# State-space input weights built in (group, channel) layout, rotation tables built by VectorE and ScalarE

## Chip, cores, metric

The kernel runs on one core of a Trainium2 chip. The metric is the device time of one execution in microseconds (us). A "piece" below is one weight tile of 128 x 1024 (or 128 x 512) floats, with the products made from it.

## What is computed

The reference is a two-layer trunk over 272 rows (16 meta tokens, 256 tokens) of 2048 features. Layer 0 mixes with a gated linear recurrence and differential attention, layer 1 with an S5 state-space layer and RWKV-7; a SwiGLU feed-forward network (hidden 5632) follows each. The change touches only constants of the S5 layer, which depend on parameters and not on the rows:

```python
dt = exp(log_dt)[:, None]                       # (64 groups, 1)
mag = exp(lr * dt)                              # (64 groups, 64 states)
ar, ai = mag * cos(li * dt), mag * sin(li * dt)
den = lr * lr + li * li
cr = ((ar - 1) * lr + ai * li) / den
ci = (ai * lr - (ar - 1) * li) / den
bbr = cr[..., None] * br - ci[..., None] * bi   # (64, 64, 16 channels): input weights
bbi = cr[..., None] * bi + ci[..., None] * br
bu_r, bu_i = einsum('btgc,gpc->btgp', ug, bbr), ... bbi
h = scan(a = ar + i ai, bu);  y = Re(c h)       # 272 rows
```

The kernel turns the complex scan into two real ones by rotating with cos(n th), sin(n th) for n = 0..271, th = li * dt. These are the rotation tables: for each of 32 blocks of 128 states a 128 x 2 x 272 tile. Tables, input weights and output weights go to one DRAM tensor, `s5p`, from which layer 1 loads one 448 KB tile per block (`stab`).

## The kernel before

Nearly all work is a stream of dense products that `run_dense` writes out in one order: layer 0's mixing, its feed-forward network (FFN0), layer 1's mixing, its feed-forward network (FFN1). For each piece, `load_piece_` has SyncE's queue (SP) load the weights (`st`), ScalarE (ACT) round them to `hi` (line 161) and VectorE (DVE) form the rest `lo` (line 162). TensorE (PE) then makes three matmuls for each of 8 (or 4) blocks: hi with xhi, hi with xlo, lo with xhi (lines 195 to 197). `st`, `hi` and `lo` have three buffers each, so `hi` of a piece can only be written once PE is through with the piece three before.

In the feed-forward network a gate product is evacuated by DVE (`ga`, line 299), passed through Silu on ACT (300) and multiplied on GpSimd (POOL, 301); the up product is multiplied with it on DVE (`gu`, 310) and split by ACT and DVE (`ah`, `al`, 214 and 215). A down product is added to `h` on DVE (210). Products have two PSUM banks: the product after next waits for the evacuation. FFN0 starts with the norm's row factors: sums of squares on PE (256), `rs` on DVE (264), the power on POOL (`rr`, 266), a broadcast copy on DVE (`re`, 268), PE (`b`, 271) and a copy on ACT (`rb`, 273).

`s5_setup` gives steps that `build` hangs on items of FFN0: `f0[2 + 6 * i]["post"] = fn`. In order: `scalars` (small DVE operations 128 x 32, lines 610 to 657), `weights_b` (POOL, 666 to 675), `weights_c` twice (POOL, 685 and 686), `weights_t` eight times and `table` eight times. `weights_t` (701 to 705) masks on POOL (`snat`), transposes on PE into PSUM bank `c` (702; 64 transposes in all), copies on ACT (`sev`) and stores. `table` (716 to 739) doubles the cos/sin table on POOL, six operations a level (`stm`, `stb`), and stores it.

Each engine runs its instructions in a fixed order, which a scheduler of the framework sets when the kernel is built from the program order, priorities and the buffers. Products' loads and evacuations have a raised priority, the tables a lowered one, so that they fill the places between.

Of the kernel before, what the change touches and what calls it, by code (L numbers as in the profile page):

```python
# [9 lines left out]
F32 = mybir.dt.float32  # L10
# [7 lines left out]
T = 272  # L18
# [15 lines left out]
for _n, _w in [  # L34
    ("g_mix0", 16), ("g_ffn0", 16), ("g_mix1", 16), ("g_ffn1", 16), ("g_fin", 16),
    ("conv_w", 32), ("conv_b", 8), ("lru_ba", 8), ("lru_bx", 8), ("lru_lam", 8), ("subln", 1),
    ("s5_d", 8), ("glu_b", 8), ("mu", 28), ("w0", 8), ("a0", 8), ("kk", 8), ("ka", 8), ("rk", 8),
    ("ln_w", 8), ("ln_b", 8), ("s5_lr", 32), ("s5_li", 32), ("s5_dt", 32),
]:
    VEC[_n] = (NV, _w)  # L40
    NV += _w


def _constants():
# [33 lines left out]
    sm = np.zeros((128, 4, 8), np.float32)  # L78
    for sc in range(4):
        for g in range(2):  # L80
            sm[64 * g:64 * g + 64, sc, 2 * sc + g] = 1
    s5 = {"sm": sm.reshape(128, 32)}
# [14 lines left out]
class Net:  # L97
# [14 lines left out]
    # ---------------------------------------------------------------- set up  # L112
# [31 lines left out]
    # ------------------------------------------------------- dense machinery  # L144
# [20 lines left out]
    def run_dense(self, items, first=(), lead=0, ahead=2):  # L165
        """The products of the items in turn; those of the first `lead` items go piece by piece through all of them."""
# [55 lines left out]
    # ------------------------------------------------------------- rms norms  # L222
# [3 lines left out]
    def norm_chunk(self, k, gname, c0):  # L226
        """h chunk k is final: scaled split of it and its part of the sum of squares."""
# [48 lines left out]
    # ------------------------------------------------------------------- FFN  # L276
# [65 lines left out]
    # --------------------------------------------------------------- layer 0  # L342
# [93 lines left out]
    def attention(self, hd, q, k, v, yb):  # L436
# [21 lines left out]
        for j, (q0, n) in enumerate(QT):  # L458
# [37 lines left out]
            # mean of squares of the normalised row, its inverse root, and the factor of the row  # L496
# [12 lines left out]
    def lru_setup(self):  # L509
# [14 lines left out]
        # softplus(-lam), twice  # L524
# [52 lines left out]
    def gelu2(self, dst, x, pl, n):  # L577
        """dst = 2 gelu(x), in the form with tanh"""
# [8 lines left out]
    # --------------------------------------------------- layer 1, state space  # L587
    def s5_setup(self):
        """Steps that make the rotations, the input and the output weights, kept in DRAM."""
# [12 lines left out]
        def scalars():  # L602
            pl = st["pl"] = self.pool("s5s", 1, es)
            st["pl2"] = self.pool("s5s2", 2, es)
            self.s5c = self.load_const("s5", pl)
            st["b"] = self.t(pl, [128, 2, 32, 16], "sb")
            st["c"] = self.t(pl, [128, 2, 32, 16], "scc")
            nc.sync.dma_start(st["b"], self.I["s5_b"])
            nc.sync.dma_start(st["c"], self.I["s5_c"])
            x = {n: self.t(pl, [128, 32], "s_" + n) for n in  # L610
                 ("dt", "th", "n", "s", "sh", "c", "ar", "ai", "den", "cr", "ci", "t")}
            self.s5_rho = self.t(self.cp, [128, 32], "s_rho")
            lr, li = self.v("s5_lr"), self.v("s5_li")
            M, A, S = ALU.mult, ALU.add, ALU.subtract
            nc.scalar.activation(x["dt"], self.v("s5_dt"), AF.Exp)
            tt(x["t"], lr, x["dt"], M)
            nc.scalar.activation(self.s5_rho, x["t"], AF.Exp)
            tt(x["th"], li, x["dt"], M)
            # the angle within one turn
            V.tensor_scalar(x["n"], x["th"], 1.0 / (2 * math.pi), 12582912.0, op0=M, op1=A)  # L620
# [4 lines left out]
            for c in (c1, c2, c3):  # L625
                V.scalar_tensor_tensor(x["th"], x["n"], -c, x["th"], op0=M, op1=A)
            pi = 3.1415925
            V.tensor_scalar(x["th"], x["th"], pi, -pi, op0=ALU.min, op1=ALU.max)
            nc.scalar.activation(x["s"], x["th"], AF.Sin)
            nc.scalar.activation(x["sh"], x["th"], AF.Sin, scale=0.5)  # L630
            tt(x["c"], x["sh"], x["sh"], M)
            V.tensor_scalar(x["c"], x["c"], -2.0, 1.0, op0=M, op1=A)
            tt(x["ar"], self.s5_rho, x["c"], M)
            tt(x["ai"], self.s5_rho, x["s"], M)
            tt(x["den"], lr, lr, M)
            tt(x["t"], li, li, M)
            tt(x["den"], x["den"], x["t"], A)
            V.reciprocal(x["den"], x["den"])
            V.tensor_scalar(x["ar"], x["ar"], 1.0, None, op0=S)
            tt(x["cr"], x["ar"], lr, M)  # L640
            tt(x["t"], x["ai"], li, M)
            tt(x["cr"], x["cr"], x["t"], A)
            tt(x["cr"], x["cr"], x["den"], M)
            tt(x["ci"], x["ai"], lr, M)
            tt(x["t"], x["ar"], li, M)
            tt(x["ci"], x["ci"], x["t"], S)
            tt(x["ci"], x["ci"], x["den"], M)
            st["x"] = x
# [668 lines left out]
```

## Time and profile before

| | us |
|---|---|
| median of 3 runs | 2692.41 |
| runs | 2690.05 to 2692.90 |
| span of the profiled execution (the only time that its page gives) | 2690.4 |
| busy in the span: PE / DVE / ACT / POOL | 2582.8 / 1663.2 / 1161.8 / 878.0 |

The page gives the busy time of each engine, the span in 40 slices with the TensorE clock granted in each, the chain that ended last, and groups of instructions by line. A matmul of 272 columns reads as some 0.29 us although the next one starts 0.125 us later, since they are pipelined; so the pace of PE is read from starts and from counts in a stretch, and its busy time only tells when it did nothing.

### The profile page before, as it was taken

The page shows a single profiled execution, that of the slowest core. Times are in us where ns is not written, and L with a number is a line of the kernel's source. Part 1 is how long each engine was busy: PE and PEld are TensorE (multiplying, and loading weights), DVE is VectorE, ACT ScalarE, POOL GpSimd, SP SyncE. Part 2 cuts the span into 40 slices and gives each one's busy share as a digit, 9 for nine tenths or more (in the row PEclk, how much of TensorE's full clock was granted, in tenths as well). Part 3 has the DMA queues.
Part 4 walks back from the last instruction along what each step waited for, and adds up shares of the span by engine and source line. Part 5 has one row for each costly group of instructions (what it writes and reads, how often), then busy time and mean ns, then how long its engine had stood idle before and what let it go on. Part 6 is the DMA issues. An engine that isn't in the chain of part 4 may idle for free. (4 is left out here: it accounts for less than half of the span.)

```text
span 2690.4 us, 50770 instructions
## 1 busy us (share of the span) xinstructions
PE 2582.8 (96%) x20136; PEld 2490.8 (93%) x20136; DVE 1663.2 (62%) x2515; ACT 1161.8 (43%) x1852; POOL 878.0 (33%) x1417
## 2 busy tenths in 40 slices
PE   8999998888899999999999989999999999999998
PEld 7999998888899999999978778799999999999997
DVE  7666767445454555556678888755755555555555
ACT  5555544333334333334444434454544434343444
POOL 3110316999831010001166776740210101010103
PEclk9999999899899999999999999999999999999999
DMA  5444455546556555555554434333555655555554
GB/s 190 141 143 142 154 177 176 172 155 215 174 183 197 177 173 175 178 173 173 186 173 150 143 121 134 98 102 117 172 188 173 190 187 185 185 188 184 185 187 143
DMA packets 160189, 447.86 MB, mean 166 GB/s; under 512 B 34960, under 2 KB 51024, under 8 KB 159824
## 3 DMA queue, kind: packets, MB, share of 16 engines
q1 hardware_dynamic: 143376, 442.32, 51.6%
q10 hardware_dynamic: 16576, 2.30, 0.5%
q8 instruction: 159, 2.61, 0.4%
q14 instruction: 78, 0.64, 0.1%
HBM read 421.69 MB, written 22.87 MB: 165 GB/s over the span
## 5 line engine op out<-in xcount | busy, mean ns | idle before, releaser
L161 ACT CAST hi<-st 128x1024 fp32r<-128x1024 f32 (+1 forms) x776 | 793.1, 1023 | 1152.1 <-PE p L196 822.1
L162 DVE TENSOR_TENSOR lo<-st,hi 128x1024 fp32r<-128x1024 f32 (+1 forms) x776 | 955.9, 1232 | 518.0 <-ACT hi L161 514.2
L195 PE MATMUL p<-xhi,hi 128*128 128x272 f32 (+1 forms) x4256 | 1238.8, 291 | 26.0 <-ACT hi L161 15.7
L197 PE MATMUL p<-xhi,lo 128*128 128x272 f32 (+1 forms) x4256 | 1239.2, 291 | 7.8 <-DVE lo L162 7.8
L196 PE MATMUL p<-xlo,hi 128*128 128x272 f32 (+1 forms) x4256 | 1235.5, 290 | 0.0
L195 PEld LDWEIGHTS p<-xhi,hi 128*128 128x128 f32 x4256 | 812.2, 191 | 39.7 <-issue 21.3
L197 PEld LDWEIGHTS p<-xhi,lo 128*128 128x128 f32 x4256 | 815.1, 192 | 21.9 <-issue 10.8
L196 PEld LDWEIGHTS p<-xlo,hi 128*128 128x128 f32 x4256 | 813.4, 191 | 11.1 <-issue 10.4
L301 POOL TENSOR_TENSOR ga<-ga,rb 128x272 f32<-128x272 f32 (+1 forms) x88 | 116.3, 1321 | 949.6 <-ACT ga L300 949.6
L195 PE MATMUL p<-ah,hi 128*128 128x272 f32 (+1 forms) x1408 | 403.3, 286 | 1.9 <-DVE gu L310 1.9
L197 PE MATMUL p<-ah,lo 128*128 128x272 f32 (+1 forms) x1408 | 403.2, 286 | 0.0
L196 PE MATMUL p<-al,hi 128*128 128x272 f32 (+1 forms) x1408 | 402.7, 286 | 0.0
L195 PEld LDWEIGHTS p<-ah,hi 128*128 128x128 f32 x1408 | 266.8, 189 | 2.1 <-issue 2.1
L197 PEld LDWEIGHTS p<-ah,lo 128*128 128x128 f32 x1408 | 266.9, 190 | 0.0
L196 PEld LDWEIGHTS p<-al,hi 128*128 128x128 f32 x1408 | 266.1, 189 | 0.0
L210 DVE TENSOR_TENSOR h<-p,h 128x256 f32<-128x256 f32 (+1 forms) x272 | 116.9, 430 | 155.6 <-PE p L197 154.6
L247 POOL TENSOR_TENSOR acc<-acc,sq 128x272 f32<-128x272 f32 (+1 forms) x56 | 60.7, 1084 | 261.8 <-ACT sq L242 261.3
L310 DVE TENSOR_TENSOR gu<-p,ga 128x272 f32<-128x272 f32 (+1 forms) x88 | 38.1, 433 | 120.2 <-PE p L197 73.9
L299 DVE TENSOR_TENSOR ga<-p,rb 128x272 f32<-128x272 f32 (+1 forms) x88 | 38.0, 432 | 54.7 <-PE p L197 54.7
L788 POOL TENSOR_TENSOR sx<-stab,sz 128x256 f32<-128x256 f32 x64 | 59.5, 932 | 26.6 <-DVE sz L785 11.0
L1078 POOL TENSOR_TENSOR xt<-ls,xs 40x15 f32<-40x15 f32 (+7 forms) x120 | 47.5, 396 | 49.5 <-DMA ls<-ld 43.1
L501 POOL TENSOR_TENSOR fs<-ss,mhalf 96x1 f32<-96x1 f32 (+1 forms) x24 | 13.3, 555 | 116.0 <-DVE ss L500 115.9
(378 smaller groups left out, 2835.6 us busy)
## 6 DMA issues: line engine op xcount, KB each, us to landing
st<-in_w_gate SPq DMA_DIRECT2D x176, 512.0 KB
st<-in_w_up SPq DMA_DIRECT2D x176, 512.0 KB
st<-in_w_down SPq DMA_DIRECT2D x160, 512.0 KB
st<-in_w_ev_in SPq DMA_DIRECT2D x80, 512.0 KB
st<-in_w_od_in SPq DMA_DIRECT2D x72, 512.0 KB
st<-in_w_ev_out SPq DMA_DIRECT2D x32, 512.0 KB
stab<-s5p SPq DMA_DIRECT2D x32, 448.0 KB
s5p<-stb SPq DMA_DIRECT2D x8, 1088.0 KB
```

The costliest lines, as they stand in the source:

```text
L161: nc.scalar.copy(hi[:, :kc], st[:, :kc])
L162: nc.vector.tensor_tensor(lo[:, :kc], st[:, :kc], hi[:, :kc].bitcast(F32), op=ALU.subtract)
L195: nc.tensor.matmul(p[:, :n], hi[:, o + k], xa, start=kk == 0, stop=False)
L196: nc.tensor.matmul(p[:, :n], hi[:, o + k], xb, start=False, stop=False)
L197: nc.tensor.matmul(p[:, :n], lo[:, o + k], xa, start=False, stop=kk == tot - 1)
L210: self.nc.vector.tensor_tensor(self.h[:, m, c0:], p, self.h[:, m, c0:], op=ALU.add)
L247: nc.gpsimd.tensor_tensor(self.acc[:, c0:], self.acc[:, c0:], sq[:, c0:], op=ALU.add)
L299: nc.vector.tensor_tensor(a[:, :n], p, self.rb[:, :n], op=ALU.mult)
L301: nc.gpsimd.tensor_tensor(a[:, :n], a[:, :n], self.rb[:, :n], op=ALU.mult)
L310: nc.vector.tensor_tensor(u[:, :n], p, a[:, :n], op=ALU.mult)
L788: (V if i == 3 else G).tensor_tensor(pr[i], a[:, NM:], b[:, NM:], op=M)
L1078: G.tensor_tensor(o, ls[:, s + 1:, s].unsqueeze(1).to_broadcast([40, j, n]), xs[:, :j, s:s + 1].to_broadcast([40, j, n]), op=M)
```

## The change

- The input weights are made in a layout of (group, channel) on the partitions and states along the row. The host lays out `lr`, `li` (repeated over the 16 channels), `br`, `bi` that way (`s5_q`, 1 MB in place of 0.5 MB), so the factors cr, ci are computed on 128 x 512 instead of 128 x 32 (`factors`), and no transpose is needed. `weights_t` is gone: its 64 transposes, 128 POOL operations, 16 ACT copies and 8 stores.
- `weights_b` masks the two groups on ACT (`seh`) and DVE (`sel`) and stores in 16 DMAs, each from 32 partitions.
- `weights_c` runs on ACT (12 activations) instead of POOL.
- The first 32 columns of all tables are made at once on DVE (`small`); each of 8 `table` steps copies them and makes the last four levels with, for each of 4 blocks, two ACT activations (`str`) and one DVE operation (`stb`).
- Steps stand 10 items apart instead of 6. Comments are removed (with that, and the new code, line numbers shift).

```diff
+        def factors():
+            x = {n: self.t(pl, [128, 512], "q_" + n) for n in ("th", "n", "s", "c", "t")}
...
+            tt(e(x["th"]), e(li), dt, M)
+            factor(x, x["th"])
+            nc.scalar.activation(x["s"], x["th"], AF.Sin)
+            nc.scalar.activation(x["th"], x["th"], AF.Sin, scale=0.5)
+            cos_of(x["c"], x["th"])
+            tt(e(x["t"]), e(lr), dt, M)
+            nc.scalar.activation(x["t"], x["t"], AF.Exp)
...
+            V.reciprocal(den, den)
...
+            nc.scalar.copy(inv, den)
...
         def weights_b():
+            for g in range(2):
+                m = hm[:, g:g + 1]
+                nc.scalar.activation(eh[:, :, :, g], bb, AF.Copy, scale=m)
+                V.scalar_tensor_tensor(el[:, :, :, g], bb, m, eh[:, :, :, g].bitcast(F32), op0=M, op1=S)
+            par = self.s5_par.rearrange("(c s) p w -> s p c w", s=4)
+            for i, x in enumerate((eh, eh, el, el)):
+                for sc in range(4):
+                    nc.sync.dma_start(par[sc, 32 * i:32 * i + 32, :, 2 * T:2 * T + 256],
+                                      x[32 * sc:32 * sc + 32].rearrange("p c m g s -> p c (m g s)").bitcast(F32))
+            st["es2"].close()
+            st["pl2"] = self.pool("s5s2", 2, es)
...
-        def weights_t(c):
-                    for sc in range(4):
...
-                            nc.gpsimd.tensor_tensor(n[:, 2 * i:2 * i + 2], src, hm, op=ALU.mult)
-                        nc.tensor.transpose(p[:, 128 * sc:128 * sc + 128], n.rearrange("p s a b -> p (s a b)"),
-                                            self.base["ident"])
-                    nc.scalar.copy(ev[:, :, m], p.rearrange("p (a b) -> p a b", a=4))
...
+        def small():
+            for lv in range(5):
+                n = 1 << lv
...
+                tt(a, co, C, M)
+                tt(b, si, Sn, M)
+                tt(tb[:, :, 0, n:2 * n], a, b, S)
+                tt(a, si, C, M)
+                tt(b, co, Sn, M)
+                tt(tb[:, :, 1, n:2 * n], a, b, A)
...
         def table(g):
-                        G.tensor_tensor(a, co, C, op=ALU.mult)
-                        G.tensor_tensor(b, si, Sn, op=ALU.mult)
...
+                tb = self.t(st["pl2"], [128, 4, 2, T], "stb")
+                V.tensor_copy(tb[:, :, :, :32], st["small"][:, 4 * g:4 * g + 4])
+                for lv, n in ((5, 32), (6, 64), (7, 128), (8, 256)):
                     w = min(n, T - n)
+                    for i in range(4):
+                        j = 4 * g + i
+                        t = self.t(st["pl2"], [128, 2, 128], "str")
+                        nc.scalar.activation(t[:, 0, :w], tb[:, i, 1, :w], AF.Copy, scale=st["nsin"][:, lv, j:j + 1])
+                        nc.scalar.activation(t[:, 1, :w], tb[:, i, 0, :w], AF.Copy, scale=st["pw"][:, lv, 1, j:j + 1])
+                        V.scalar_tensor_tensor(tb[:, i, :, n:n + w], tb[:, i, :, :w], st["pw"][:, lv, 0, j:j + 1],
+                                               t[:, :, :w], op0=M, op1=A)
...
-        steps += [weights_t(c) for c in range(8)] + [low(table(g)) for g in range(8)]
+        steps = [scalars, factors, weights_b, weights_c(0), weights_c(1), small]
+        steps += [low(table(g)) for g in range(8)]
...
-                f0[2 + 6 * i]["post"] = fn
+                f0[2 + 10 * i]["post"] = fn
```

How the order of instructions moves, at three places. The first is DVE's queue in FFN0 from the norm's broadcast copy `re` on (`lo` belongs to the weight pieces; `s_`, `spw` are 128 x 32 values of `scalars`). Before:

```order
L268 COPY re<-rr 68x512
L600 TENSOR_TENSOR s_t<-s_ai,vec 128x32
L600 TENSOR_TENSOR s_ci<-s_ai,vec 128x32
L632 TENSOR_SCALAR s_c<-s_c 128x32
L600 TENSOR_TENSOR s_ar<-s_rho,s_c 128x32
L651 COPY spw<-s_c 128x32
```

Now (`q_` are the 128 x 512 values of `factors`, `stq` and `stm` belong to `small`), and, some 60 instructions later, the reciprocal:

```order
L266 COPY re<-rr 68x512
L598 TENSOR_TENSOR q_th<-sq_5266,q_dt 128x512
L598 TENSOR_TENSOR q_t<-sq_5266,q_dt 128x512
L598 TENSOR_TENSOR s_t<-spw 128x32
...
L160 TENSOR_TENSOR lo<-st,hi 128x1024
L598 TENSOR_TENSOR stq<-stm_7944,stm_7945 128x32x4
L670 TENSOR_SCALAR q_c<-q_c 128x512
L669 RECIPROCAL q_n<-q_n 128x512
L598 TENSOR_TENSOR q_th<-q_s,sq_5266 128x512
L160 TENSOR_TENSOR lo<-st,hi 128x1024
```

Operations sixteen times as wide, and the steps of `small`, now stand between the `lo` of consecutive pieces; it goes on so for 22 pieces.

The second place is SP's queue, where the input weights are stored. Before, one of the eight stores among the weight loads:

```order
L158 DMA st<-in_w_down 128x512 x9
L705 DMA s5p<-sev 128x4x256
L158 DMA st<-in_w_down 128x512 x6
L739 DMA s5p<-stb 128x4x544
```

Now, all sixteen, in FFN0's second slice:

```order
L708 DMA s5p<-seh 32x8x256 x2
L156 DMA st<-in_w_up 128x1024
L708 DMA s5p<-seh 32x8x256 x6
L708 DMA s5p<-sel 32x8x256 x2
L156 DMA st<-in_w_up 128x1024
L708 DMA s5p<-sel 32x8x256
L156 DMA st<-in_w_gate 128x1024
L708 DMA s5p<-sel 32x8x256 x2
L156 DMA st<-in_w_gate 128x1024
L708 DMA s5p<-sel 32x8x256 x3
L156 DMA st<-in_w_up 128x1024 x2
```

The stores that were spread over FFN0 now stand together, with four weight loads among them.

The third place is DVE's queue in FFN0's first down product, whose pieces are 128 x 512 (`h` is the evacuation of a product). Before:

```order
L162 TENSOR_TENSOR lo<-st,hi 128x512
L210 TENSOR_TENSOR h<-p,h 128x272
L162 TENSOR_TENSOR lo<-st,hi 128x512
L210 TENSOR_TENSOR h<-p,h 128x272
```

Now, at its eleventh to thirteenth evacuation:

```order
L160 TENSOR_TENSOR lo<-st,hi 128x512
L755 SCALAR_TENSOR_TENSOR stb<-stb,spw,str 128x2x64
L208 TENSOR_TENSOR h<-p,h 128x272
L755 SCALAR_TENSOR_TENSOR stb<-stb,spw,str 128x2x64
L747 COPY stb<-stq 128x8x32
L755 SCALAR_TENSOR_TENSOR stb<-stb,spw,str 128x2x64
L208 TENSOR_TENSOR h<-p,h 128x272
L755 SCALAR_TENSOR_TENSOR stb<-stb,spw,str 128x2x128 x2
L208 TENSOR_TENSOR h<-p,h 128x272
L160 TENSOR_TENSOR lo<-st,hi 128x512
```

Table operations, each waiting for ACT, now stand between `lo` and `h`, and once the evacuations of the 11th, 12th and 13th product stand ahead of the `lo` of the 14th.

## Rows read from the trace of the kernel before

**Rows 1.** Busy time by stretch: FFN0's first 2496 matmuls, its other 3840; FFN1's start.
```profile
core 0: us, PE busy (x) PEld busy (x) DVE busy (x) ACT busy (x) POOL busy (x), PEclk, DMA share, GB/s
412.86:803.80 390.94, 346.94 (x2584) 342.19 (x2583) 207.20 (x267) 137.55 (x177) 315.77 (x619) 0.93 0.56 180
803.80:1286.37 482.57, 482.57 (x3845) 482.57 (x3843) 266.07 (x311) 195.31 (x239) 49.95 (x41) 1.00 0.56 178
1919.95:2058.28 138.33, 138.33 (x1164) 138.33 (x1165) 73.58 (x88) 59.87 (x77) 18.49 (x15) 1.00 0.55 176
2082.58:2173.95 91.37, 91.37 (x768) 91.37 (x769) 49.41 (x56) 38.72 (x48) 11.72 (x8) 1.00 0.61 191
```
**Rows 2.** Waits 412.86:803.8 of PE, DVE, SP: total us, times, longest.
```profile
PE c L702 <- POOL snat L701: 18.1, 7, 6.1
PE p L195 <- ACT hi L161: 7.1, 2, 4.9
...
PE b L271 <- DVE re L268: 4.8, 1, 4.8
...
DVE gu L310 <- POOL ga L301: 45.0, 10, 8.3
...
SPq L739 <- POOL stb L735: 26.3, 4, 9.1
```
**Rows 3.** PE in order of time, after the norm: start, us, instruction.
```profile
421.97 0.28 PE L196 MATMUL p<-xlo,hi 128*128 128x272 f32 x1
427.03 1.95 PE L271 MATMUL b<-c_base,re 68*128 68x68 f32 x8 [4.78 <-DVE re L268]
428.73 0.57 PE L197 MATMUL p<-xhi,lo 128*128 128x272 f32 x1
...
431.15 0.43 PE L195 MATMUL p<-xhi,hi 128*128 128x272 f32 x1
431.57 0.29 PE L197 MATMUL p<-xhi,lo 128*128 128x272 f32 x1
```
**Rows 4.** The same stretch on DVE, POOL and ACT.
```profile
416.31 0.35 DVE L638 RECIPROCAL s_den<-s_den 128x32 f32<-128x32 f32 x1
419.77 7.12 DVE L268 COPY re<-rr 68x512 f32<-68x512 f32 x1 [0.29 <-POOL rr L266]
428.10 1.23 DVE L162 TENSOR_TENSOR lo<-st,hi 128x1024 fp32r<-128x1024 f32 x1
429.25 0.18 DVE L600 TENSOR_TENSOR s_cr<-s_cr,s_den 128x32 f32<-128x32 f32 x1
...
419.71 6.89 POOL L685 TENSOR_TENSOR scw<-scc,c_base 128x256 f32<-128x256 f32 x12
...
417.55 1.28 ACT L629 ACT_TABLE_LOAD   x1
418.84 0.23 ACT L629 ACTIVATE s_s<-s_th 128x32 f32<-128x32 f32 x1
```
**Rows 5.** Instructions of line 268: duration in ns, min/median/max.
```profile
L268 DVE COPY re<-rr x5: 293/424/7116, 36.8 to 2677.8; 68x512 f32<-68x512 f32 x3, 128x256 f32<-128x256 f32 x2
```
**Rows 6.** Groups by line over the span: count | busy us, mean ns.
```profile
L300 ACT ACTIVATE ga<-ga 128x272 f32<-128x272 f32 x44 | 18.8, 428 | 15.0 <-DVE ga L299 15.0
L162 DVE TENSOR_TENSOR lo<-st,hi 128x512 fp32r<-128x512 f32 x48 | 34.4, 716 | 10.8 <-ACT hi L161 9.1
L210 DVE TENSOR_TENSOR h<-p,h 128x272 f32<-128x272 f32 x128 | 56.2, 439 | 78.1 <-PE p L197 77.8
L702 PE MATMUL c<-c_base,snat 128*128 128x128 f32 x64 | 16.8, 296 | 18.3 <-POOL snat L701 18.1 <-POOL stb L717 0.2
```
**Rows 7.** Busy time in a stretch of 2 us, columns as in the first group.
```profile
724.00:726.00 2.00, 2.00 (x11) 2.00 (x10) 0.00 (x0) 0.59 (x1) 0.87 (x4) 0.50 1.02 311
```
**Rows 8.** ACT's casts in 412.86:803.8 by shape: count | busy us, mean ns.
```profile
L161 ACT CAST hi<-st 128x1024 fp32r<-128x1024 f32 x96 | 100.5, 1049 | 153.4 <-PE p L196 93.3 <-DMA st<-in_w_up 17.4 <-DMA st<-in_w_gate 17.1
L161 ACT CAST hi<-st 128x512 fp32r<-128x512 f32 x16 | 9.9, 621 | 20.6 <-PE p L196 12.6 <-DMA st<-in_w_down 5.5 <-DVE lo L162 0.9
```

More of the change, by code (lines that the diff above doesn't have):

```diff
@@ L597, in s5_setup, with factor @@
         V = nc.vector
+        M, A, S = ALU.mult, ALU.add, ALU.subtract
         def tt(o, a, b, op):
             V.tensor_tensor(o, a, b, op=op)
[L602 to L620, printed above, removed]
+        def factor(x, th):
+            V.tensor_scalar(x["n"], th, 1.0 / (2 * math.pi), 12582912.0, op0=M, op1=A)
             V.tensor_scalar(x["n"], x["n"], 12582912.0, None, op0=S)
@@ new lines, in scalars @@
+        def scalars():
+            pl = st["pl"] = self.pool("s5s", 1, es)
+            st["es2"] = ExitStack()
+            st["plq"] = self.pool("s5q", 1, st["es2"])
+            self.s5c = self.load_const("s5", pl)
+            st["c"] = self.t(pl, [128, 2, 32, 16], "scc")
+            nc.sync.dma_start(st["c"], self.I["s5_c"])
+            st["q"] = self.t(st["plq"], [128, 4, 512], "sq4")
+            nc.sync.dma_start(st["q"], self.I["s5_q"])
+            x = {n: self.t(pl, [128, 32], "s_" + n) for n in ("dt", "th", "n", "sh", "t")}
+            self.s5_rho = self.t(self.cp, [128, 32], "s_rho")
+            lr, li = self.v("s5_lr"), self.v("s5_li")
+            pw = st["pw"] = self.t(pl, [128, 9, 2, 32], "spw")
+            nc.scalar.activation(x["dt"], self.v("s5_dt"), AF.Exp)
+            tt(x["t"], lr, x["dt"], M)
+            nc.scalar.activation(self.s5_rho, x["t"], AF.Exp)
+            tt(x["th"], li, x["dt"], M)
+            factor(x, x["th"])
+            nc.scalar.activation(pw[:, 0, 1], x["th"], AF.Sin)
+            nc.scalar.activation(x["sh"], x["th"], AF.Sin, scale=0.5)
+            cos_of(pw[:, 0, 0], x["sh"])
@@ new lines, in weights_b @@
+        def weights_b():
+            pl = st["plq"]
+            bb = st["bb"]
+            hm = self.s5c["hq"]
+            eh = self.t(pl, [128, 8, 2, 2, 64], "seh", F32R)
+            el = self.t(pl, [128, 8, 2, 2, 64], "sel", F32R)
+            for g in range(2):
[9 more added lines that the diff above has]
+            st["pl2"] = self.pool("s5s2", 2, es)
@@ L686, in f @@
-                nc.gpsimd.tensor_scalar(cw[:, :, 2], cw[:, :, 2], -1.0, None, op0=ALU.mult)
+                        sg = self.base["hm"][:, g:g + 1] if i < 2 else self.s5c["hn"][:, g:g + 1]
+                        nc.scalar.activation(cw[:, :, i, g], st["c"][:, m, 16 * half:16 * half + 16], AF.Copy, scale=sg)
                 nc.sync.dma_start(self.s5_par[16 * half:16 * half + 16, :, 2 * T + 256:].rearrange("j p c -> p j c"),
@@ L740, in f @@
+                nc.sync.dma_start(self.s5_par[4 * g:4 * g + 4, :, :2 * T].rearrange("j p c -> p j c"),
                                   tb.rearrange("p j a t -> p j (a t)"))
             return f
-        steps = [scalars, weights_b, weights_c(0), weights_c(1)]
         def low(fn):
```

153 lines of the change are left out of this document (61 added, 92 removed).

## Prediction

> **What bounds the kernel now.** I read the table by stretch first [rows 1]. PE sets the end: in FFN0's later 3840 matmuls it is busy in all of 482.57 us, 0.1257 us a matmul, at a granted clock of 1.00, while DVE works 266 us and ACT 195 us of it. Nothing off PE counts there. The same network's first 2496 matmuls, the stretch in which the state-space constants are made, take 390.94 us. At 0.1257 they would take 313.7. So **77.3 us** are lost, and that is all the change can reach. In it POOL is busy 316 of 391 us, PE idles 390.94 - 346.94 = 44.0 us, and the clock is 0.93.
>
> Then the waits of that stretch [rows 2]. PE waits longest for `snat`, the masks that POOL makes for the transposes (18.1 us). The others look like DVE or ACT being late, but POOL is behind them: DVE stood 45.0 us before `gu`, for the Silu product that POOL had queued behind table operations, and SP stood 26.3 us before a table's store, with weight loads queued behind it.
>
> Third, one stall in order of time [rows 3, 4]. PE stops for 4.78 us at the norm's row factors until DVE's `re` is there. `re` took 7.12 us, from 419.77, while POOL ran twelve operations from 419.71 for 6.89 us; its median is 0.424 us [rows 5]. [...]
>
> **The change part by part.** *Removed:* transposes, masks and tables on POOL, thus every wait in [rows 2] that ends on POOL, the slow `re`, and SP's wait for POOL. I take all 77.3 us as gone and add back what takes its place. Five terms.
>
> 1. The norm at FFN0's start. FFN1 has the same norm with nothing beside it: its first 1152 matmuls take 138.33 us where 1152 x 91.37 / 768 = 137.1 are plain [rows 1]. So 1.3 us are the floor. ACT now loads function tables three times there instead of twice, and does the exponential of `q_t` ahead of `rb`. A load took 1.28 us, and the activation behind it started right at its end [rows 4]. I take 2 us; ends 1.3 and 5.
>    [...]
>
> 2. `factors` and `small` on DVE, over 22 pieces, 22 x 24 x 0.1257 = 66 us of PE. Old work there: `lo` 1.23 us a piece and, every four pieces, `ga`, `gu` and `al`, each about as long as the evacuation `h` of the same shape, 0.44; together 34 us. To that come some 40 small steps of `scalars` at 0.18, 7 us [rows 4, 6]. New: about 30 operations of 512 columns, between half of a 1024-column `lo` and the 128 x 512 one, 0.61 to 0.72 us, 20 us; two of 1024 columns, 2.5; 30 steps of `small` from 0.18 to 0.72, 11; and the reciprocal. A 128 x 32 reciprocal took 0.35 against 0.18 of a product, 0.17 more for 32 columns, so about 3.3 us at 512 [rows 4]. Sum 78 us by durations. But each instruction starts about 0.08 us before the one ahead ends (428.10 + 1.23 against 429.25 [rows 4]), and there are some 150: 66 us. DVE then just keeps PE's pace, with the reciprocal as its worst lump. DVE normally finishes a piece's `lo` 6.0 - 1.05 - 1.23, or 3.7 us, before PE needs it. So between 0 and (78 - 66) - 3.7 + 1.2 = 9.5 us; I take 3, since the overlap is plain in the rows.
>
> 3. The sixteen stores. The first waits for `seh`, which ACT writes in about 2.5 us behind the `hi` of FFN0's 24th piece, 1.05 us, once PE is through with the 21st. The load behind the last store is the 31st piece's. PE then has pieces 22 to 30, 9 x 3.02 = 27.1 us, less 3.6 and less `hi` and `lo` of the 31st, 2.3: 21.2 us. To move in it: 16 x 32 x 8 x 256 x 4 bytes = 4.19 MB and four loads of 0.52, 6.29 MB. With its DMA engines full the kernel moved 311 GB/s [rows 7], which gives 20.3 us. It just fits; I take 1 us. DVE's first table copy waits for these stores too, with the same piece's `lo` behind it: the same deadline. Ends 0 and, at half that rate for the stores, 14 (below). SP's sixteen issues stand only beside its own slack.
>
> 4. FFN0's first down product. The `lo` of its 14th product now stands behind the evacuation of the 13th, so PE must stop: 0.44 + 0.72 us [rows 6], less two matmuls that need only `hi`, plus 1.2 at half clock: 2 us.
>
> 5. The rest of the table steps, 54 pieces (38 long, 16 short: 138 us of PE). ACT: casts 38 x 1.05 + 16 x 0.62 = 50 us [rows 8], 19 Silu and `ah` at 0.43, 8 us; and 256 new activations of 16 to 128 columns. Nearest rows: 0.23 us at 32 columns [rows 4], 0.43 at 272 [rows 6]; by width (60 columns in the mean) 0.25, 65 us. Sum 123 of 138 us. At 0.43 it would be 168, 30 too many. DVE has 136 short operations there, about 30 us, beside some 70 of its own. What may cost is the chain DVE to ACT to DVE, each link behind a `hi` that waits for PE. I take 3 us; ends 0 and 30.
>
> Layer 1's tail is reordered a little by the scheduler with the same instructions: 0, ends -4 and +4. Free POOL time elsewhere is worth nothing. Sum of what comes back: 2 + 3 + 1 + 2 + 3 = 11. **Gain 77.3 - 11 = 66 us.** The span was 2690.4, inside the range of the runs and 2.0 under their median, so I subtract from the median: 2692.4 - 66 = **2626 us**.
>
> **Rivals.** *The stores are slow.* Their source is 32 partitions, not 128. If such a transfer moves at half of 311 GB/s, the stores take 27.0 us and the loads among them 6.8, 33.8 against 21.2: PE stands 12.6 us, and 1.2 more at half clock, 13 above the 1 counted: 2639. Against it: two or more of them are under way at once, from different partitions. [...] Chance 0.14.
>
> *ACT becomes the bound in the table steps*, by term 5 at up to 30 us, less the 3 counted: up to 2653, likelier half of it, 2640. For it: 256 activations and their waits. Against: 0.23 us is the nearest row. Chance 0.13.
>
> *Slower.* The same chain, if it decides: to lose the 77 us the 54 pieces would need 138 + 77 = 215 us of ACT, less 58 for the old work, so 0.61 us for each of the 256 activations, waits included; above that the kernel is slower than before. At 0.65 it is 2692 - 66 - 3 + (58 + 166 - 138) = 2709. Rows at 0.23 and 0.43 speak against it. Chance 0.03.
>
> *The change doesn't free PE*: the weight stream, and not POOL, makes the early waits (ACT's `hi` waited 34.5 us for loads [rows 8]), and only the `snat` waits (18.1 us) and the transposes, at most their 16.8 us [rows 6], go: 2692 - 35 = 2657. Against it: the DMA share is 0.56 in both stretches of FFN0 [rows 1], with no wait in the later. Chance 0.04; nothing gained at all, 0.01.
>
> **The numbers.** My forecast has 0.65. Its own range goes from the floor (only 1.3 us come back, layer 1 gains 4: 2692 - 76 - 4 = 2612) to terms 2 and 3 at their ends. The range 2612 to 2656 takes in both rivals that end faster and leaves out the slower one, half of the last and some of the tails. No change means within 0.2%, 5.4 us, which a measurement of this kernel can hardly tell apart. Faster 0.96, same 0.01, slower 0.03, from the cases above.
>
> **What would show it.** Right: FFN0's first 2496 matmuls in 320 to 330 us, clock above 0.97, POOL nearly idle, no wait before `gu` on POOL, `re` at 0.4 us, one short PE stop in the first down product. Term 2 wrong: PE waiting for `lo` some 12 pieces into FFN0, behind the reciprocal. Term 3 wrong: one long stop near the 31st piece, with ACT waiting for a load or DVE for a store. Term 5 wrong: many short stops with DVE waiting for `str`. The forecast as a whole is wrong if FFN0's later 3840 matmuls change, or if layer 1 shifts by more than 4 us.

## The result

The changed kernel takes **2627.89 us** (median of 4 runs, 2625.61 to 2631.55) beside 2691.23 us of the kernel before in the same comparison: ratio 0.9773, 95% interval 0.9758 to 0.9789. The forecast was 2626 us, in a range of 2612 to 2656. The profiled execution has a span of 2624.0 us, 66.4 under that of before.

The two traces laid side by side, by the starts of the dense matmuls:

| stretch | before, us | changed, us | difference |
|---|---|---|---|
| up to FFN0 | 412.9 | 413.4 | +0.5 |
| FFN0's first 2496 matmuls | 390.9 | 331.7 | **-59.2** |
| FFN0's other 3840 | 482.6 | 484.2 | +1.7 |
| layer 1's mixing | 633.6 | 627.2 | -6.4 |
| FFN1 to the end of the span | 770.4 | 767.5 | -2.9 |

The changed kernel's busy time by stretch, columns as in [rows 1]; the rows answer to its first, second, third and fourth, with layer 1's mixing between:

```profile
413.38:745.09 331.71, 323.99 (x2522) 321.33 (x2521) 240.79 (x452) 198.72 (x437) 29.72 (x23) 0.98 0.67 217
745.09:1229.32 484.23, 484.23 (x3843) 484.23 (x3842) 266.00 (x311) 194.71 (x238) 49.61 (x38) 1.00 0.53 174
1229.32:1856.49 627.17, 598.20 (x4322) 527.23 (x4321) 476.08 (x776) 286.23 (x576) 340.49 (x597) 0.98 0.45 139
1856.49:1994.15 137.66, 137.66 (x1164) 137.66 (x1165) 73.59 (x88) 59.86 (x77) 18.44 (x15) 1.00 0.54 177
2018.43:2109.36 90.93, 90.93 (x769) 90.93 (x769) 49.41 (x56) 38.45 (x48) 11.70 (x8) 1.00 0.59 192
```

In the first row POOL's 315.77 us are down to 29.72, PE idles 331.71 - 323.99 = 7.7 us instead of 44.0, and the clock is 0.98 instead of 0.93. DVE and ACT carry the work, and PE doesn't notice it, but for four places. The waits of PE and DVE in this stretch (total, times, longest; against [rows 2]):

```profile
PE p L195 <- DVE lo L160: 4.1, 4, 2.5
PE p L193 <- ACT hi L159: 3.4, 3, 2.6
...
DVE stb L747 <- DMA s5p<-stb: 2.7, 2, 1.9
DVE stb L755 <- ACT str L754: 2.2, 6, 0.5
...
DVE gu L308 <- POOL ga L299: 1.0, 2, 0.7
```

The 45.0 us before `gu` have become 1.0. The norm's copy is back at its usual length (against [rows 5]), and PE has no stop there:

```profile
L266 DVE COPY re<-rr x5: 294/423/424, 35.7 to 2612.0; 68x512 f32<-68x512 f32 x3, 128x256 f32<-128x256 f32 x2
```

**Where the rest lies.** The stretch still takes 331.7 - 313.7 = 18 us more than its matmuls. Cut at PE's stops:

```profile
413.38:449.50 36.12, 35.95 (x288) 35.14 (x287) 31.35 (x83) 24.79 (x41) 6.44 (x3) 1.00 0.73 233
449.50:460.00 10.50, 8.01 (x52) 7.79 (x51) 10.50 (x22) 3.48 (x5) 1.79 (x1) 0.84 0.41 122
...
500.00:513.00 13.00, 9.95 (x56) 9.41 (x55) 3.56 (x5) 3.99 (x5) 0.77 (x1) 0.74 1.01 331
...
591.00:594.00 3.00, 2.21 (x15) 1.77 (x15) 2.98 (x8) 2.80 (x8) 0.00 (x0) 1.00 0.34 131
594.00:610.00 16.00, 14.78 (x113) 14.12 (x112) 11.60 (x26) 12.40 (x36) 0.77 (x1) 1.00 0.89 301
```

A row counts the matmuls under way, two or three more than start in it. From the starts: the norm 36.12 - 261 x 0.1257 (its 24 small matmuls left out) = 3.3 us; the stop at 450, 10.5 - 49 x 0.1257 = 4.3; the one at 502, 13 - 54 x 0.1257 = 6.2; the first down product 1.4; behind it 2.0; the stretches left out and the last 135 us together 0.8. Two stops make more than half of it. In the row from 449.50 DVE is busy all the time; in that from 500.00 the DMA engines are (share 1.01).

The first, on DVE in order of time:

```profile
445.73 1.21 DVE L160 TENSOR_TENSOR lo<-st,hi 128x1024 fp32r<-128x1024 f32 x1
446.86 0.28 DVE L598 TENSOR_TENSOR stq<-stm,stm 128x128 f32<-128x128 f32 x1
447.07 0.41 DVE L670 TENSOR_SCALAR q_c<-q_c 128x512 f32<-128x512 f32 x1
447.40 3.34 DVE L669 RECIPROCAL q_n<-q_n 128x512 f32<-128x512 f32 x1
...
451.51 1.21 DVE L160 TENSOR_TENSOR lo<-st,hi 128x1024 fp32r<-128x1024 f32 x1
```

PE's matmul with that second `lo` starts at 452.77, 2.77 us behind the one ahead of it. The second stop, on SP's queue (an SP row's duration is the time that the queue spent on issuing):

```profile
487.97 0.82 SPq L708 DMA_DIRECT2D s5p<-seh  x2
488.89 0.55 SPq L156 DMA_DIRECT2D st<-in_w_up  x1
489.49 6.46 SPq L708 DMA_DIRECT2D s5p<-seh  x6
496.05 1.85 SPq L708 DMA_DIRECT2D s5p<-sel  x2
497.99 0.71 SPq L156 DMA_DIRECT2D st<-in_w_up  x1
498.75 1.11 SPq L708 DMA_DIRECT2D s5p<-sel  x1
499.96 0.42 SPq L156 DMA_DIRECT2D st<-in_w_gate  x1
500.43 1.40 SPq L708 DMA_DIRECT2D s5p<-sel  x2
501.93 0.61 SPq L156 DMA_DIRECT2D st<-in_w_gate  x1
502.58 2.63 SPq L708 DMA_DIRECT2D s5p<-sel  x3
```

The sixteen stores occupy SP for 0.82 + 6.46 + 1.85 + 1.11 + 1.40 + 2.63 = 14.3 us. The load issued at 497.99, behind ten of them, is that of FFN0's 28th piece; its `hi` on ACT:

```profile
504.24 1.04 ACT L159 CAST hi<-st 128x1024 fp32r<-128x1024 f32 x1 [3.54 <-DMA st<-in_w_up]
```

PE starts that piece at 505.33, 2.90 us after its last matmul of the 27th.

### The profile page after: what moved, and what is told of

Its sections match the earlier page's. It is cut to its first block, busy times and chain, and to the rows that moved or that the text cites. A ratio compares the mean times of both kernels' runs of the same rounds, so it can differ in the third digit from the quotient of the medians.

```text
span 2624.0 us, 50534 instructions
## 1 busy us (share of the span) xinstructions
PE 2558.7 (98%) x20072; PEld 2467.8 (94%) x20072; DVE 1698.1 (65%) x2700; ACT 1221.0 (47%) x2111; POOL 591.2 (23%) x820
## 5 line engine op out<-in xcount | busy, mean ns | idle before, releaser
L160 DVE TENSOR_TENSOR lo<-st,hi 128x1024 fp32r<-128x1024 f32 (+1 forms) x776 | 936.4, 1207 | 489.8 <-ACT hi L159 485.8
L299 POOL TENSOR_TENSOR ga<-ga,rb 128x272 f32<-128x272 f32 (+1 forms) x88 | 126.1, 1433 | 1231.5 <-ACT ga L298 1231.5
L806 POOL TENSOR_TENSOR sx<-stab,sz 128x256 f32<-128x256 f32 x64 | 63.5, 995 | 27.6 <-DVE sz L803 10.5
L218 DVE SCALAR_TENSOR_TENSOR xlo<-h,vec,xhi 128x272 fp32r<-128x272 f32 (+1 forms) x64 | 50.7, 800 | 0.6 <-ACT xhi L217 0.5
```

Source lines behind the costliest of these rows:

```text
L160: nc.vector.tensor_tensor(lo[:, :kc], st[:, :kc], hi[:, :kc].bitcast(F32), op=ALU.subtract)
L218: nc.vector.scalar_tensor_tensor(lo, src, g, hi.bitcast(F32), op0=ALU.mult, op1=ALU.subtract)
L299: nc.gpsimd.tensor_tensor(a[:, :n], a[:, :n], self.rb[:, :n], op=ALU.mult)
L806: (V if i == 3 else G).tensor_tensor(pr[i], a[:, NM:], b[:, NM:], op=M)
```

## The experiments

Stretches are those of the table above, each from one profile (two where there are two numbers); each ratio is to the kernel before in the same comparison.

| run | FFN0's first 2496 | layer 1's mixing | median, us | ratio, 95% interval |
|---|---|---|---|---|
| before; again (one run) | 390.9; 388.9 | 633.6; 632.5 | 2691.2; 2687.8 | 1 |
| tables only | 338.3 | 637.1 | 2642.9 | 0.9829 (0.9805 to 0.9852) |
| weights only | 375.3 | 635.4 | 2675.6 | 0.9953 (0.9936 to 0.9969) |
| weights_c only | 384.2 | 627.3 | 2681.5 | 0.9974 (0.9965 to 0.9984) |
| ga on VectorE | 399.0 | 634.6 | 2697.4 | 1.0027 (1.0009 to 1.0046) |
| changed; again | 331.7; 327.9 | 627.2; 631.1 | 2627.9; 2627.0 | 0.9773; 0.9774 (0.9753 to 0.9794) |
| no reciprocal | 328.6 | 637.0 | 2626.4 | 0.9764 (0.9748 to 0.9781) |
| reciprocal spread; again | 324.6; 325.7 | 638.7; 634.5 | 2629.9; 2630.3 | 0.9779; 0.9778 (0.9764 to 0.9794) |
| fewer stores | 323.3 | 641.6 | 2631.4 | 0.9785 (0.9772 to 0.9799) |
| spread and fewer stores | 323.9 | 639.5 | 2630.8 | 0.9783 (0.9769 to 0.9797) |
| activations twice | 330.2 | 629.2 | 2626.2 | 0.9765 (0.9750 to 0.9780) |

### One part of the change at a time

Tables only: `small` and `table` of the changed kernel in the kernel before (`weights_c`'s tile moves with them to the pool with one buffer).

```diff
-        steps = [scalars, weights_b, weights_c(0), weights_c(1)]
+        steps = [scalars, weights_b, weights_c(0), weights_c(1), small]
...
         steps += [weights_t(c) for c in range(8)] + [low(table(g)) for g in range(8)]
```

> Only the tables go to VectorE and ScalarE; masks, transposes and weights_c stay as before. Theory (GpSimd's one queue is the jam, and tables and masks share in it): the waits of gu and of SP's stores on GpSimd go, the 18.1 us at snat shrink to about half, the transposes and the slow re stay; FFN0's first 2496 matmuls take 349 to 369 us instead of 391, the kernel 22 to 42 us less than before. Rival 1 (masks and transposes make nearly all of the loss): at most 15 us less. Rival 2 (the tables make nearly all of it): 55 us less or more.

Measured: -52.6 us in the stretch (against the second profile of before -50.6), -46.6 in the median; between the theory's range and the second rival's. The tables made most of the loss. PE's waits there:

```profile
PE p L197 <- DVE lo L162: 6.2, 4, 4.7
PE p L195 <- DVE gu L310: 2.1, 1, 2.1
PE p L195 <- ACT hi L161: 1.0, 1, 1.0
PE c L705 <- POOL snat L704: 1.0, 2, 0.9
```

Masks and transposes are all still there, and the 18.1 us of [rows 2] at `snat` are 1.0. So the masks were late because of the table operations on POOL, in whose queue they stood. The expectation was wrong on `re`: it took 0.42 us here, with `weights_c` still on POOL (below).

Weights only: the changed kernel with `table` of the kernel before and without `small`.

```diff
-        steps = [scalars, factors, weights_b, weights_c(0), weights_c(1), small]
+        steps = [scalars, factors, weights_b, weights_c(0), weights_c(1)]
```

> Only the input and output weights are made the new way; the tables stay on GpSimd, 10 items apart. Theory: the snat waits (18.1 us), the transposes (about 10) and the slow re (6) go, the norm, the reciprocal and the stores cost some 9 of it again, and gu still waits for GpSimd: 20 to 40 us less than before, FFN0's first 2496 matmuls in 351 to 371 us. Rival 1 (masks and transposes make nearly all of the loss): 50 us less or more. Rival 2 (the tables do): at most 10 us less.

Measured: -15.7 us in the stretch, -13.9 in the median, under the theory's range and above the second rival's. The parts overlap little: 52.6 + 15.7 = 68 against the 57 to 63 of the whole; by the medians 46.6 + 13.9 = 60.5 against 62.5. This run also shows how POOL slows DVE. One `lo`, in order of time, and the busy time of its stretch:

```profile
522.21 13.61 DVE L160 TENSOR_TENSOR lo<-st,hi 128x1024 fp32r<-128x1024 f32 x1
```
```profile
522.19:535.75 13.56, 2.28 (x19) 2.06 (x17) 13.56 (x3) 2.41 (x3) 12.55 (x18) 0.66 0.00 0
```

The operation takes 1.21 to 1.23 us elsewhere. POOL ran eighteen table operations without a pause beside it, and PE stood for some 11.4 of the 13.6 us. The kernel before does the same. Its second profile has this, with `ga` on POOL in the middle of the train:

```profile
546.44 12.58 DVE L162 TENSOR_TENSOR lo<-st,hi 128x1024 fp32r<-128x1024 f32 x1 [1.61 <-ACT hi L161]
```

PE waited 7.4 us for it. In the profile shown ahead the longest `lo` of this stretch is 2.06 us: where such a hold falls changes from one execution to the next.

Weights_c only, in the kernel before:

```diff
-                        nc.gpsimd.tensor_tensor(cw[:, :, i, g], src[:, :, g], hm[:, :, g], op=ALU.mult)
-                nc.gpsimd.tensor_scalar(cw[:, :, 2], cw[:, :, 2], -1.0, None, op0=ALU.mult)
+                        sg = self.base["hm"][:, g:g + 1] if i < 2 else self.s5c["hn"][:, g:g + 1]
+                        nc.scalar.activation(cw[:, :, i, g], st["c"][:, m, 16 * half:16 * half + 16], AF.Copy, scale=sg)
```

> The kernel before, with weights_c alone on ScalarE, so that the twelve 128 x 256 operations no longer run on GpSimd beside re. Theory (re took 7.12 us because GpSimd's long operations ran back to back beside it): re takes under 1.5 us, the pause at the norm goes, 4 to 8 us less than before. Rival (whatever GpSimd runs next holds re as long): re stays above 3 us and the gain is 0 to 3 us.

Measured: -6.8 us in the stretch against the first profile of before and -4.7 against the second, -7.9 in the median; `re` is back at 0.42 us:

```profile
419.89 0.42 DVE L268 COPY re<-rr 68x512 f32<-68x512 f32 x1 [0.28 <-POOL rr L266]
```

POOL's next operations had 4 columns here. The theory's numbers are met, but this run can't credit them to `re`: the second profile of the kernel before, `weights_c` on POOL as ever, has `re` at 0.42 us too, with the stop at the norm gone:

```profile
418.94 0.42 DVE L268 COPY re<-rr 68x512 f32<-68x512 f32 x1 [0.29 <-POOL rr L266]
419.34 8.12 POOL L685 TENSOR_TENSOR scw<-scc,c_base 128x256 f32<-128x256 f32 x12 [0.44 <-DMA scc<-in_s_c]
```

There POOL waited 0.44 us for a load, so its twelve operations began 0.40 us behind `re`; they took 8.12 us instead of 6.89. Where they began 0.06 us ahead of it ([rows 4], and the run with `ga` on VectorE below), `re` took 7.12 and 7.19 us. So what held `re` was a train of long POOL operations that had begun before it, and that one stop comes and goes between executions; the whole stretch was only 2 us shorter without it. At 431.8 of this run PE waits 4.67 us for `ga`. The gain of 7.9 us in the median is clear of the noise (ten executions against fourteen); which of POOL's fewer operations brings it isn't shown.

### Is it POOL's queue, or POOL beside DVE?

```diff
-                nc.gpsimd.tensor_tensor(a[:, :n], a[:, :n], self.rb[:, :n], op=ALU.mult)
+                (nc.gpsimd if layer else nc.vector).tensor_tensor(a[:, :n], a[:, :n], self.rb[:, :n], op=ALU.mult)
```

> The kernel before, with the product behind FFN0's Silu (ga) on VectorE instead of GpSimd, and all constants still made on GpSimd. Theory (the loss is the wait in GpSimd's queue: 45 us of VectorE before gu): these waits go, PE's stops at hi, gu, ga and lo shrink, 15 to 30 us less than before. Rival (the loss is GpSimd's operations holding VectorE's up while they run): ga is held up on VectorE too, 0 to 8 us less.

Measured: 8 us *more* in the stretch, 0.3% slower in the median of ten executions. All 45 us of waiting before `gu` for POOL are gone, and nothing is won on the whole. One `lo`, and the stretch in which it ran:

```profile
471.91 25.28 DVE L162 TENSOR_TENSOR lo<-st,hi 128x1024 fp32r<-128x1024 f32 x1 [0.56 <-ACT hi L161]
```
```profile
471.91:497.11 25.20, 5.22 (x42) 5.00 (x40) 25.20 (x1) 2.39 (x3) 25.20 (x36) 0.67 0.04 17
```

POOL was busy in all of 25.20 us with table operations, and DVE couldn't finish one subtraction; PE waited 20.1 us for it. Without this one stop the stretch would be some 10 us shorter than before's, so what the queue's waits gave was taken back by the hold, in this execution by one hold; the ten executions lie 24 us apart (2682.25 to 2706.19), the profiled one at 2701.68. Whether moving `ga` made holds of this length likelier isn't shown, as the kernel before has one of 12.58 us itself. The rival was nearer, and too mild. So taking work off POOL has two effects: what waits in its queue comes earlier (the 45.0 us before `gu` are 1.0 in the changed kernel), and DVE is no longer held (`lo` takes 1228 ns there in the mean, 1388 before). The second can't be had by moving `ga` alone: `lo` took 1579 ns here.

### The two stops that are left

Reciprocal in four pieces, each behind another `gu` (the part of `factors` ahead of it joins the step of `scalars`, the rest becomes a step of its own):

```diff
-            V.reciprocal(den, den)
...
+                d = den[:, 128 * i:128 * i + 128]
+                V.scalar_tensor_tensor(d, self.gu[:, :128], 0.0, d, op0=M, op1=A)
+                V.reciprocal(d, d)
```

> The changed kernel with the 128 x 512 reciprocal cut into four of 128 x 128, each made to follow another evacuation of an up product (by adding 0 times gu to its input), so that two lo stand between them. Theory (the 2.77 us stop some 12 pieces into FFN0 comes from the reciprocal's 3.34 us as one lump on VectorE): the stop and the half clock behind it go, 3 to 4 us less than the changed kernel, FFN0's first 2496 matmuls in 324 to 329 us. Rival (VectorE has too much to do in these 22 pieces as a whole): stops of 2 us or more remain among pieces 8 to 22, and the time changes by less than 1.5 us.

Measured: behind the norm no gap between starts of 0.5 us or more among the first 35 pieces, the stretch 324.6 us (again 325.7): the lump was it, and not DVE's work as a whole. The stop at the stores, which now come later, is shorter too (gaps of 0.5 to 1.0 us near 530). But the whole is no faster: the median is 2 to 3 us above the changed kernel's, within the intervals.

Stores once each, from 128 partitions, to a tensor of their own; layer 1 loads four bands:

```diff
-            for i, x in enumerate((eh, eh, el, el)):
-                for sc in range(4):
...
+            for i, x in enumerate((eh, el)):
+                nc.sync.dma_start(self.s5_bw[i], x.rearrange("p c m g s -> p c (m g s)").bitcast(F32))
...
-        nc.sync.dma_start(tb, self.s5_par[j])
+        nc.sync.dma_start(tb[:, 256:], self.s5_par[j])
+        for i in range(4):
+            nc.sync.dma_start(tb[32 * i:32 * i + 32, :256], self.s5_bw[i // 2, 32 * sc:32 * sc + 32, c])
```

> The changed kernel with seh and sel stored once each, in two transfers from 128 partitions to a DRAM tensor of their own (2.1 MB instead of 4.2 MB in sixteen transfers from 32 partitions); layer 1 loads the four bands of 32 partitions by four more transfers for each block. Theory (the stop of 3 to 4 us near the 30th piece comes from the burst of stores that fills the DMA engines): it goes with its half clock, 4 to 5 us less than the changed kernel, and layer 1's mixing stays within 625 to 635 us. Rival (the stop is SP's order, weight loads behind stores, whatever their size): a stop of 2 us or more remains there. Second rival: layer 1 pays for its 128 more transfers, over 637 us.

Measured: the stop is gone, the stretch 323.3 us. So the first rival fell. The queue now spends 0.33 us on each of two stores:

```profile
485.18 0.33 SPq L707 DMA_DIRECT2D s5bw<-seh  x1
...
488.64 0.33 SPq L707 DMA_DIRECT2D s5bw<-sel  x1
```

But layer 1's mixing took 641.6 us, and the whole is not faster. Part of that is the second rival's: PE there waits for the new transfers, and never for `stab` in the changed kernel. The rest of the difference is within what layer 1 varies by (below).

```profile
PE c L791 <- DMA stab<-s5bw: 4.8, 3, 2.3
```

Both edits:

> Both edits together, the reciprocal in four pieces and the input weights stored once. Theory (the two stops are separate): 7 to 9 us less than the changed kernel, 2617 to 2622 us, FFN0's first 2496 matmuls in 320 to 324 us. Rival (one stop moves to the next late thing): 0 to 4 us less.

Measured: 323.9 us in the stretch, no better than one of them, with stops of 1.0, 1.6 and 1.0 us near 590 instead, at a clock of 0.86 from 588 to 600; layer 1 at 639.5, 4.6 us of it PE's wait for the new transfers; 2630.8 us. The theory failed on the sum: with the two stops gone the first down product loses more (some 5.6 us by the starts; 3.4 and 2.4, with the pieces just behind it, in the changed kernel), and layer 1 pays again.

No reciprocal, for what the stop is worth alone:

```diff
-            V.reciprocal(den, den)
```

> The changed kernel without its 128 x 512 reciprocal: the factors are multiplied by the denominator instead of its inverse, so the state-space input weights are not the reference's. The order of all other instructions of every engine but VectorE's neighbours of it stays, layer 1's included. Theory (the stop at the reciprocal is worth 3 to 4 us, and layer 1 took 7 to 10 us more in the three kernels before only because its instructions were put in another order): FFN0's first 2496 matmuls in 324 to 328 us, layer 1's mixing in 626 to 636, the kernel 2622 to 2626 us. Rival (what FFN0 gains, layer 1 loses, whatever the order): layer 1's mixing above 636 and no gain.

Measured: the stop at 450 is gone (behind the norm no gap over 0.5 us before 495.9), the stretch is 328.6 us, just outside the theory's range and inside the two profiles of the changed kernel (327.9 and 331.7); the stop at the stores stayed, 2.67 and 1.01 us. The median is 0.6 to 1.5 us lower, which can't be told from nothing. And layer 1 took 637.0 us with the order of instructions that took 627.2 and 631.1 elsewhere, so the order alone doesn't make such a difference. This profile is of the slowest of its four executions (2632.97 us, the others 2625.91 to 2626.84): what it says of layer 1, for the theory or the rival, is one execution's.

The reciprocal spread once more, for layer 1:

> The changed kernel with the reciprocal in four spread pieces, once more. Theory (layer 1's 638.7 us there comes from the order that the scheduler gave it, above all in the matmuls from the 1872nd to the 2184th of its 2496, which took 73 us against 61 to 63): layer 1's mixing in 635 to 642 us again, that part in 70 us or more. Rival (it was one execution among others): anywhere between 627 and 636, that part in 61 to 68.

Measured: 634.5 us and 69.8 in the part named (layer 1 has 2688 such matmuls, not the 2496 of the expectation), a hair outside the theory's numbers and outside the rival's for the part. The rows show that the part isn't the same work: 546 matmuls here (first row), 496 in the changed kernel's second profile (second row).

```profile
1709.45:1779.24 69.79, 66.64 (x546) 65.42 (x544) 41.63 (x74) 35.63 (x74) 25.26 (x55) 0.98 0.38 113
```
```profile
1710.87:1773.26 62.39, 60.84 (x496) 60.09 (x496) 41.12 (x71) 33.28 (x67) 16.43 (x39) 0.97 0.35 117
```

Whether that order costs layer 1 anything stays open; one program's layer 1 varies by as much (below).

### How near is ScalarE to binding?

```diff
                         nc.scalar.activation(t[:, 0, :w], tb[:, i, 1, :w], AF.Copy, scale=st["nsin"][:, lv, j:j + 1])
+                        nc.scalar.activation(t[:, 0, :w], tb[:, i, 1, :w], AF.Copy, scale=st["nsin"][:, lv, j:j + 1])
+                        nc.scalar.activation(t[:, 1, :w], tb[:, i, 0, :w], AF.Copy, scale=st["pw"][:, lv, 1, j:j + 1])
```

> The changed kernel with each of the 256 activations of the table steps done twice (the second overwrites the first with the same values). By the rows that is some 85 us more of ScalarE by durations; the scheduler spreads the table steps over 74 pieces where there were 50. Theory (ScalarE's time beyond PE's pace is added to the end, the mechanism of the rival that ends slower): some 200 us of ScalarE in pieces that take PE 175, 20 to 45 us more than the changed kernel, 2647 to 2672 us. Rival (the spread takes it up, ScalarE doesn't bind): at most 8 us more.

Measured: no effect. The stretch takes 330.2 us, between the two of the changed kernel, though ACT works 58 us more in it:

```profile
413.86:744.07 330.21, 323.18 (x2522) 321.26 (x2521) 241.95 (x452) 256.67 (x693) 34.96 (x24) 0.98 0.67 216
```

The last table activation starts at 733 us instead of 654: the lowered priority let the steps move on to later pieces.

### Controls

> The changed kernel again, on the same chip. 60 to 68 us less than before. If the scheduler's reordering made layer 1's mixing 6.4 us shorter, it takes 625 to 629 us again; if that was the difference between two executions, it may lie anywhere between 625 and 635.

> The kernel before, profiled once more: FFN0's first 2496 matmuls within 389 to 393 us, the other 3840 in 482.6. If layer 1's mixing varies between executions of one program, it may take 627 to 636 us here (633.6 in the profile shown); if it doesn't, 633 to 634.

Measured: the changed kernel gives the same ratio, with layer 1 at 631.1 us, so not at 625 to 629 again; its first stretch varies by 4 us between two profiles (51 starts at half clock in one, 27 in the other). The kernel before gives 388.9 and 632.5. Four profiles in which PE has the changed kernel's order in layer 1 (changed twice, weights only, no reciprocal) show 627.2, 631.1, 635.4 and 637.0 us there. A difference of under 10 us in layer 1 between two profiles therefore says nothing.

## Why the prediction was right, point by point

**The bound and its size: right.** What the change could reach was the 77.3 us of FFN0's first 2496 matmuls, and 57 to 63 went (two profiles of either kernel; the second of before loses 75.2). The waits for POOL in that stretch come to 1.0 us before `gu` and 0.9 before `re`, `re` is at 0.42 us, the clock at 0.98 to 0.99.

**Why they were lost: half right.** The prediction has POOL behind `gu`, `snat` and SP as a queue, and POOL beside DVE only at `re`. The runs show the second in every kernel with tables on POOL. DVE's `lo` and `al` in that stretch, before (L162, L215) and in the changed kernel (L160, L213):

```profile
L162 DVE TENSOR_TENSOR lo<-st,hi 128x1024 fp32r<-128x1024 f32 x96 | 133.1, 1388 | 75.8 <-ACT hi L161 75.7
L215 DVE TENSOR_TENSOR al<-gu,ah 128x272 fp32r<-128x272 f32 x20 | 15.1, 754 | 0.0
```
```profile
L160 DVE TENSOR_TENSOR lo<-st,hi 128x1024 fp32r<-128x1024 f32 x96 | 117.9, 1228 | 48.6 <-ACT hi L159 48.3
L213 DVE TENSOR_TENSOR al<-gu,ah 128x272 fp32r<-128x272 f32 x20 | 8.7, 433 | 0.0
```

`lo` took 1388 ns in the mean against 1228, `al` 754 against 433; `gu` and `ga`, which read PSUM, took 440 and 435 ns before and 439 and 437 after. `lo` and `al` read two tiles in SBUF, but `re`, a copy with one input, was held too (7.12 us against 0.42). Why POOL held these and not `gu` and `ga` is not shown. 18 and 36 of POOL's instructions went by before DVE's one `lo` was through, after 13.61 and 25.28 us. `snat`, the longest wait of PE, was the tables' doing (1.0 us once they were gone). How the tables' 52.6 us divide between queue and holds no run separates. The prediction's third reading, the stop at the norm, is right for its profile and chance as a part of the loss: the second profile doesn't have it.

**Term 1, the norm** (2 us): 3.3 and 2.4 in the two profiles, counted up to the stop of the reciprocal. No stop; three table loads on ACT, 1.28 us each (at 422.38, 424.98 and 428.15), are hidden: PE waits for nothing from 412 to 432, and the activation behind each load starts within 0.02 us of its end.

**Term 2, the reciprocal** (3 us): 4.3 and 2.8. Its length was estimated at 3.3 us and is 3.34; the stop is 12 pieces into FFN0, where the prediction put it. That is the sign it gave for this term being wrong, and it came at the size that the term has. Spread, the reciprocal costs nothing.

**Term 3, the stores** (1 us): **6.2 and 5.8. This is the term that was mis-sized.** The failing step is "The load behind the last store is the 31st piece's", with its budget of 21.2 us. The load that came late is that of the 28th piece, behind ten stores; PE needed it some 14 us after the first store. The next wrong step is "SP's sixteen issues stand only beside its own slack": they held SP for 14.3 us, so the load wasn't even issued until 497.99. The rival of slow stores asks for their rate. The changed kernel while most of the sixteen stores ran, columns as in [rows 1]:

```profile
490.00:504.00 14.00, 12.72 (x101) 12.50 (x100) 4.70 (x6) 3.18 (x5) 2.25 (x2) 1.00 1.02 280
```

and the kernel with two stores from 128 partitions, while these ran:

```profile
486.00:496.00 10.00, 10.00 (x82) 10.00 (x81) 7.36 (x10) 3.28 (x7) 2.31 (x1) 1.00 0.99 370
```

The DMA engines are full in both, at 280 and at 370 GB/s, loads among the stores included. So less is moved beside the sixteen stores, by some quarter; no run shows the half of the rate that the rival, and the end of 14 us for this term, assume; of the rival's 13 us more some 5 came. That the 32 partitions do it is not shown: the sixteen stores also write rows of 1 KB (8 x 256 floats from each partition), the two write 8 KB from each in one piece. How much of the stop is partitions, rows, bytes or SP's time the runs don't separate: one edit took away all four.

**Term 4, the first down product** (2 us): 1.4, in front of the `hi` and the `lo` of the 14th product, as forecast. The prediction's sums have 1.2 us at half clock for a new stall here, in term 2 and in the rival of slow stores. No run shows one such price. The slow starts cost 1.2 us behind the norm's stop of before (clock 0.51 from 428.73 to 431.57). In the changed kernel they cost 1.4 behind the stop at 450 (14 starts in the 3.17 us from 453.79), 2.1 behind the one at 502 (21 in the 4.76 us from 506.99), and nothing behind these two short stops: the clock is 1.00 in the row from 591.00 and in the next.

**Term 5, the other table steps** (3 us): 2.0 behind the down product and less than 1 elsewhere. The activations took 293 to 394 ns, not the estimated 250. It didn't matter, and the arithmetic of the two rivals on ACT (chances 0.13 and 0.03) was wrong in another way: it held the steps to 54 pieces, while the scheduler moves them on when ACT has more to do. Twice the activations cost nothing.

**The sum.** The terms came to 18 and 14 us instead of 11, 3 to 7 of gain less than forecast. In the profile shown that is made up by layer 1's -6.4, which is not shown to be an effect of the change: its order gave 627 to 637 us. So it is partly luck that the profiled span fell by 66.4, the very gain forecast; the medians fell by 63.3 and 62.5. "0, ends -4 and +4" for layer 1 was right in the mean (632.7 of four profiles in the new order, 633.1 of two of before) and too narrow for two single profiles. FFN0's +1.7 and FFN1's -2.9 don't come from a wait (below). By the prediction's last test it would be wrong as a whole if FFN0's later 3840 matmuls changed. They did, by the same 1.67 us in every profile with the new weights; the prediction has no term for it, and its cause is open. It is small beside the range. The prediction's 320 to 330 us for the first stretch were met by one profile of the changed kernel (327.9) and missed by the other (331.7).

**The spacing of the steps, 10 items instead of 6**, is worth nothing: built with 6, the changed kernel has the same instructions in the same order on every engine.

## What to carry to other kernels

- An engine off the critical path can hold another up while it runs, as POOL held DVE here (a `lo` of 1.2 us took 12.58 to 25.28): look for an instruction whose longest duration is many times its median, in more than one profile, and see what runs beside it; a queue's waits and such holds look alike in a table of waits, and only a run that moves one of them tells which it is.
- For a burst of DMA issues on one queue, check the deadline of each load among them, the first above all, and count the queue's own issue time (14.3 us here), not only the bytes.
- A stop of 3 to 5 us that is taken away in a kernel whose later stage varies by 10 us can be read only from its own stretch; three versions that won 2 to 8 us there were no faster as a whole, and none tried is better than the changed kernel.

## What was not expected of the hardware

- POOL's back-to-back operations held a 1.2 us DVE subtraction for 13.61 us (18 operations) and for 25.28 us (36), and in the kernel before for 12.58 us: the hold didn't end between two of POOL's instructions. POOL's own operations vary too; whether DVE holds them was not tried. POOL's `ga` takes some 0.75 us in the middle of a train of its own, and 878 ns in the mean of the stretch before; where POOL comes to it from a pause, it takes more: 1378 ns in the changed kernel's stretch (first row), and as much in FFN0's other 3840 of the kernel before (second row), where DVE works little more than half of the time. The longest in the second profile of the changed kernel (third row) ran beside a train of six DVE operations.

```profile
L299 POOL TENSOR_TENSOR ga<-ga,rb 128x272 f32<-128x272 f32 x20 | 27.6, 1378 | 241.9 <-ACT ga L298 241.9
```
```profile
L301 POOL TENSOR_TENSOR ga<-ga,rb 128x272 f32<-128x272 f32 x24 | 35.6, 1483 | 340.1 <-ACT ga L300 340.1
```
```profile
476.99 4.51 POOL L299 TENSOR_TENSOR ga<-ga,rb 128x272 f32<-128x272 f32 x1 [10.59 <-ACT ga L298]
```

- The same matmuls without any wait have a pace of their own in each program. FFN0's other 3840 took 482.56 us in every kernel with the old input weights and GpSimd's tables, 483.46 with the new tables alone, and 484.23 in all that have the new weights. By the starts the whole difference lies in the gate and up products; the 1536 matmuls of the down products take 193.7 us in each. FFN1 to the end took 769.5 to 770.4 us with the old weights and 766.9 to 768.0 with the new, but for one profile of 770.6. The granted clock is 1.00 in FFN0's stretch of each. What sets it was not tried.
